# Modulation by per-column sums on VectorE, and unread matmuls on TensorE in three places of a two-model transformer kernel

## The chip, the cores and the metric

The kernel runs on one core of a Trainium2 chip. The metric is the device time of one execution in microseconds; for repeated executions the median is given. Before the change it is 2462.95 us, the median of three runs between 2461.41 and 2464.72 us.

## The reference, cut to what matters

The input is one sequence of 512 positions with 1024 features. It goes through a first model of two layers (banded attention, a gated short convolution, a SwiGLU feed-forward of width 2816) and then through one layer of a second model, here called the second block. That layer is modulated by a vector `c`:

```
c_act = jax.nn.silu(c)                              # c: 1 x 1024
mod = c_act @ ada_w[l] + ada_b[l]                   # ada_w: 1024 x 6144
sh_a, sc_a, gt_a, sh_m, sc_m, gt_m = split(mod, 6)
h = rmsnorm(x, norm_mix_g[l]) * (1.0 + sc_a) + sh_a
proj = h @ w_in[l]
```

`mod` depends on `c` and `ada_w` alone, so it can be computed at any time before the second block. It is 48 columns of 128 values in the kernel's layout.

## The kernel before

**Tiling.** Activations stand features by positions: 128 features on the partitions, 512 positions in a row. Every weight matrix is cut into units of 128 x 1024 (512 KB), 382 in all. A unit is loaded as `raw` on the queue of SyncE (line 255), cast by ScalarE to its high half `wh` (line 267), and VectorE subtracts to get the low half `wl` (line 268). `mm_kb` multiplies in three matmuls: high x high, high x low, low x high (lines 523 to 525). A unit serves 24 matmuls of 512 columns. `Stream.next` splits two units ahead of use. All of these tiles come from one pool, `blkp`, of 39 buffers; PSUM has eight banks, handed out in a fixed cycle by `ps`.

**Order.** The program lists its steps; a scheduler orders each engine's instructions by program order and by simulated times, and each engine then executes its list in order, waiting where data is missing. `order` (line 374 uses it for table loads) adds a dependency without a semaphore.

**Modulation.** `ada_start` computes silu(c) at the start from small VectorE instructions and one Exp. `ada_step` is called twice in each of the iterations 2 to 13 of the first model's feed-forward loop, in both layers, 48 times in all. Each step loads the next block of `ada_w` (128 rows of one sixth, 512 KB, `adaraw`, line 934) and multiplies the present one by a scalar per partition, adding into `adaacc` (lines 918 and 920). After every eighth step, eight matmuls with the tile of ones as moving operand sum `adaacc` over the partitions (line 927; each is executed as two passes, one column each), and VectorE adds the bias into `mod` (line 930).

**The crossing.** Between two stages that need a norm over all features, `cross` works in two halves of 256 positions: `tail(0)`, `chain(0)`, `tail(1)`, then the first half's normalised input, `chain(1)`, and `Head`, the first matmuls of the next stage, half by half. For the second block the chain is `chain2`: `rstd` sums squares over the partitions with one-column matmuls (tile `pc`, line 416), GpSimd takes the power -0.5, `bcast` spreads the result with one matmul against a diagonal (tiles `dg`, `pb`, lines 427 and 431), the residual is added and squared, and `rstd` and `bcast` run a second time for the pre-norm. PE has little else to do while a half's chain runs. `b2_masks` loads constants (line 968) and casts them on VectorE (line 971, tile `pastr`) right after the crossing in program order.

**The start.** `setup` issues the first loads and sets a 128 x 128 tile of ones (line 357). PE's first instruction comes when the first weight unit and input block are loaded and split.

Of the kernel before, what the change touches and what calls it, by code (L numbers as in the profile page):

```python
# [14 lines left out]
P = 128  # L15
T = 512
D = 1024
NB = 8
# [14 lines left out]
def col_layout():  # L33
    off, lay = 0, {}

    def add(name, n):
        nonlocal off
        lay[name] = (off, n)
        off += n

    for l in range(DEPTH):
        for n in ("g_pre_mix", "g_post_mix", "g_pre_ffn", "g_post_ffn"):
            add(f"{n}{l}", NB)
        add(f"conv_w{l}", 3 * NB)
        add(f"sink{l}", NH)
    for n, c in (("c", NB), ("ada_b", 48), ("nmg", NB), ("nfg", NB), ("fcw", 3 * NF), ("fcb", NF), ("dgq", 1),
                 ("dgk", 1), ("lam", P), ("subg", 1), ("fgq", 1), ("fgk", 1), ("fbf", 4), ("ngq", 1), ("ngk", 3),
                 ("pe", 32)):
        add(n, c)
    return lay, off  # L50
# [32 lines left out]
def pack(inp):  # L83
# [47 lines left out]
    for l in range(DEPTH):  # L131
# [4 lines left out]
    setc("c", fm_cols(inp["c_2"][0]))  # L136
# [39 lines left out]
    for i in range(2):  # L176
# [20 lines left out]
        "ada": np.asarray(inp["ada_w_2"])[0].reshape(NB, P, 6, U).transpose(2, 0, 1, 3).reshape(48, P, U),  # L197
# [82 lines left out]
class Kern:  # L280
# [31 lines left out]
    def small(self, name, shape, dt=F32, bufs=3):  # L312
        return self.smp.tile(shape, dt, name=self.n(name), tag=name, bufs=bufs)

    TAIL = 4
    NHF = 4
    NH3 = 4
# [20 lines left out]
    def setup(self):  # L338
        nc = self.nc
        self.cols = self.cpool.tile([P, self.ncol], F32, name="cols")  # L340
        nc.sync.dma_start(self.cols[:, :NB], self.a["cols"][:, :NB])
        xin = self.a["x"].rearrange("p (j a t) -> p j a t", j=4, a=2)
        self.xsrc = [[xin[:, j, :, t0:t1] for j in range(4)] for t0, t1 in HV]
        self.xpre = {}
        self.st.load_to(1)
        for j in range(4):
            self.xpre[0, j] = self.xload(0, j)
        self.st.load_to(3)
        self.cst = self.cpool.tile([P, 520], F32, name="cst")
        nc.sync.dma_start(self.cst, self.a["consts"])  # L350
        nc.sync.dma_start(self.cols[:, NB:], self.a["cols"][:, NB:])
        self.ident = self.cst[:, 0:P]
        self.band = self.cst[:, P:512]
        self.caus = self.cst[:, 384:512]
        self.valid = self.cst[:, 512:520]
        self.ones = self.cpool.tile([P, P], F32, name="ones")
        nc.vector.memset(self.ones, 1.0)
        self.mhalf = self.cpool.tile([P, 4], F32, name="mhalf")
        nc.vector.memset(self.mhalf, -0.5)
        self.R = self.cpool.tile([P, T], F32, name="R")  # L360
# [47 lines left out]
    def rstd(self, acc, hv, acc_tail=None):  # L408
        nc = self.nc
        n = (hv[1] - hv[0]) // P  # L410
        pc = self.ps("pc")
        parts = [acc[:, a, hv[0]:hv[1]] for a in range(2)] if len(acc.shape) == 3 else [acc[:, hv[0]:hv[1]]]
        parts += acc_tail if acc_tail else []
        for j, a in enumerate(parts):
            for i in range(n):
                nc.tensor.matmul(pc[:, i:i + 1], a[:, i * P:(i + 1) * P], self.ones[:, 0:1],
                                 start=j == 0 and i == 0, stop=j == len(parts) - 1 and i == n - 1)
        v = self.small("rs_v", [P, 4])[:, :n]
        r = self.small("rs_r", [P, 4])[:, :n]
        nc.vector.tensor_scalar(v, pc[:, :n], 1.0 / D, EPS, op0=OP.mult, op1=OP.add)  # L420
        self.rstd_small(v, r, n)
        return r

    def bcast(self, r, n=4):
# [6 lines left out]
        nc.tensor.matmul(pb[:, :n * P], self.ones, dg[:, :n * P], start=True, stop=True)  # L431
        return pb

    def add_sq(self, acc, src, first, eng):
# [24 lines left out]
        self.nc.sync.dma_start(d, t)  # L459
        self.xdst[hi][j] = d  # L460

    def cross(self, tail, chain, head, fin, early=0):
        self.xdst = [[None] * 4 for _ in range(2)]
        if tail:
            tail(0)
# [1 line left out]
        post0 = chain(0)  # L467
        if tail:
            tail(1)
        post0()  # L470
        post1 = chain(1)
        head.run(0)
# [45 lines left out]
    def mm_kb(self, ps, w, h, kb, first, last, wk=None, hv=(0, T)):  # L518
# [6 lines left out]
        nc.tensor.matmul(ps[:, t], w[1][:, sl], h.hi[kb][:, t], start=False, stop=last)  # L525

    def mblock(self, h):
        w = self.st.next()
# [364 lines left out]
        return F  # L893

    def ada_start(self):
        nc = self.nc
        self.ca = self.cpool.tile([P, NB], F32, name="ca")
        o, _ = self.lay["c"]
        c = self.cols[:, o:o + NB]
        self.sigmoid_small(self.ca, c, [P, NB])  # L900
        nc.vector.tensor_mul(self.ca, self.ca, c)
        self.mod = self.cpool.tile([P, 48], F32, name="mod")
        self.ada_i = 0
        self.ada_raw = None

    def ada_step(self):
        nc = self.nc
        i = self.ada_i
        if i >= 48:
            return  # L910
        self.ada_i += 1
        if i == 0:
            self.ada_load(0)
        t = self.ada_raw
        g, kb = divmod(i, NB)
        if kb == 0:
            self.ada_acc = self.blk("adaacc", [P, U], F32)
            nc.vector.tensor_scalar(self.ada_acc, t, self.ca[:, 0:1], None, op0=OP.mult)
        else:
            nc.vector.scalar_tensor_tensor(self.ada_acc, t, self.ca[:, kb:kb + 1], self.ada_acc, op0=OP.mult,  # L920
                                           op1=OP.add)
        if i + 1 < 48:
            self.ada_load(i + 1)
        if kb == NB - 1:
            ps = self.ps("ada")
            for m in range(NB):
                nc.tensor.matmul(ps[:, m:m + 1], self.ada_acc[:, m * P:(m + 1) * P], self.ones[:, 0:1], start=True,
                                 stop=True)
            o = self.lay["ada_b"][0] + g * NB
            nc.vector.tensor_add(self.mod[:, g * NB:(g + 1) * NB], ps[:, :NB], self.cols[:, o:o + NB])  # L930

    def ada_load(self, i):
        self.ada_raw = self.blk("adaraw", [P, U], F32)
# [45 lines left out]
    def chain2(self, i, pend, h, G, sh, xs=None, acc2=None, sq2=None):  # L979
# [3 lines left out]
        if pend:  # L983
# [10 lines left out]
        pb = self.bcast(self.rstd(acc2, HV[i], sq2), 2)  # L994
        R = self.half("Rp")
        nc.scalar.copy(R, pb[:, :256])

# [194 lines left out]
    def block2(self, tail, pend):  # L1192
# [5 lines left out]
        self.cross(tail, lambda i: self.chain2(i, pend, h, self.G1, 0, acc2=acc2), head, lambda i: None)  # L1198
        self.b2_masks()
        o = FM(self, "o2", NB, F32)  # L1200
        lo_h, hi_h = slice(0, 64), slice(64, 128)
# [580 lines left out]
```

## Time and profile before

| | us |
|---|---|
| median of three runs | 2462.95 |
| lowest, highest | 2461.41, 2464.72 |
| the profiled execution | 2465.88 |
| its span, first to last instruction | 2464.2 |
| PE busy in it | 2407.3 |
| DVE busy in it | 1324.1 |
| ACT busy in it | 996.1 |
| POOL busy in it | 399.2 |

PE is TensorE's matmuls, PEld its weight loads, DVE VectorE, ACT ScalarE, POOL GpSimd, SP SyncE, on whose queue all loads stand. A busy time is the union of an engine's instructions. A matmul's duration is that of one instruction from issue to its end; since matmuls overlap in the array, the distance between two starts is the time that one takes from the stream. A clock of 1.00 is the granted TensorE clock of 2.4 GHz, 0.50 that of 1.2 GHz. Times in the traces count from the span's start.

### The profile page before, as it was taken

The numbers are of one execution on the slowest core, as the hardware profiler recorded it, in microseconds if no ns is written. First come the engines' busy times: TensorE is split into PE (matmuls) and PEld (weight loads), VectorE is DVE, ScalarE is ACT, GpSimd is POOL, SyncE is SP. The second block draws the span as 40 slices with busy tenths as digits, with TensorE's granted clock in tenths as the row PEclk, the third lists the DMA queues.
The fourth block names the chain that finished last, engine by engine and source line by source line (L and its number), as shares of the span: only waits on it lengthen the run. The fifth ranks groups of instructions, "written<-read, shape, count | busy, mean of one in ns | idle before, by whom it ended". The sixth has DMA issues, their size and how long they took to land.

```text
span 2464.2 us, 32671 instructions
## 1 busy us (share of the span) xinstructions
PE 2407.3 (98%) x12680; PEld 2073.7 (84%) x12680; DVE 1324.1 (54%) x2324; ACT 996.1 (40%) x1808; POOL 399.2 (16%) x437
## 2 busy tenths in 40 slices
PE   8999999999999999999999999999898899999999
PEld 8888888888888898888888888888788878888888
DVE  6777544366533177775434655422667586644531
ACT  4555423442223245554224322322375575333420
POOL 3433001211110034230012111100021232000000
PEclk9999999999999999999999999999799999999999
DMA  4511523355423244223233553332221204233350
GB/s 159 149 61 64 165 94 103 103 196 200 149 85 121 80 144 126 69 83 99 94 98 129 181 195 137 99 107 74 91 88 53 83 22 146 78 103 103 105 171 24
DMA packets 90115, 272.77 MB, mean 111 GB/s; under 512 B 10175, under 2 KB 19007, under 8 KB 89960
## 3 DMA queue, kind: packets, MB, share of 16 engines
q1 hardware_dynamic: 89960, 270.68, 33.1%
q8 instruction: 100, 1.64, 0.3%
q14 instruction: 55, 0.45, 0.1%
HBM read 249.65 MB, written 15.22 MB: 107 GB/s over the span
## 4 chain that ended last, share of the span: by engine, by line
PE 90%; DVE 3%; ACT 3%; POOL 2%; issue 2%; DMA 0%; SPq 0%; POOLq 0%; ACTq 0%; DVEq 0%
PE ps L523 24%; PE ps L525 24%; PE ps L524 24%; PE hd L524 2%; PE hd L525 2%; PE hd L523 2%; PE o L840 2%; PE pt L815 1%; PE tm L1025 1%; PE tm L1026 1%; PE tm L1027 1%; POOL t L576 1%; POOL t L575 1%; ACT pp L378 1%; PE s L791 1%
## 5 line engine op out<-in xcount | busy, mean ns | idle before, releaser
L268 DVE TENSOR_TENSOR wl<-raw,wh 128x1024 fp32r<-128x1024 f32 x382 | 477.5, 1267 | 346.6 <-ACT wh L267 283.2
L267 ACT CAST wh<-raw 128x1024 fp32r<-128x1024 f32 x382 | 390.0, 1050 | 188.6 <-DMA raw<-in_w_dram 99.0
L525 PE MATMUL ps<-hh,wl 128*128 128x512 f32 x752 | 295.3, 393 | 0.9 <-DVE wl L268 0.8
L524 PE MATMUL ps<-hl,wh 128*128 128x512 f32 x752 | 294.9, 392 | 0.0
L523 PE MATMUL ps<-hh,wh 128*128 128x512 f32 x752 | 294.4, 392 | 0.0
L524 PE MATMUL ps<-hfl,wh 128*128 128x512 f32 x640 | 249.3, 390 | 0.0
L523 PE MATMUL ps<-hfh,wh 128*128 128x512 f32 x640 | 249.1, 390 | 0.0
L525 PE MATMUL ps<-hfh,wl 128*128 128x512 f32 x640 | 248.9, 389 | 0.0
L525 PEld LDWEIGHTS ps<-hh,wl 128*128 128x128 f32 x752 | 141.3, 188 | 29.1 <-DVE wl L268 2.1
L524 PEld LDWEIGHTS ps<-hl,wh 128*128 128x128 f32 x752 | 141.2, 188 | 27.2
L523 PEld LDWEIGHTS ps<-hh,wh 128*128 128x128 f32 x752 | 141.2, 188 | 27.1 <-ACT ot L844 0.2
L525 PE MATMUL ps<-hidh,wl 128*128 128x512 f32 (+1 forms) x396 | 145.1, 366 | 0.0
L523 PE MATMUL ps<-hidh,wh 128*128 128x512 f32 (+1 forms) x396 | 144.9, 366 | 0.0
L524 PE MATMUL ps<-hidl,wh 128*128 128x512 f32 (+1 forms) x396 | 144.7, 365 | 0.0
L378 ACT ACTIVATE pp<-pp,at_nm 128x256 f32<-128x256 f32 (+1 forms) x208 | 114.4, 553 | 68.2 <-DVE at_nm L797 60.0
L525 PEld LDWEIGHTS ps<-hfh,wl 128*128 128x128 f32 x640 | 120.1, 188 | 24.9
L524 PEld LDWEIGHTS ps<-hfl,wh 128*128 128x128 f32 x640 | 120.2, 188 | 24.7
L523 PEld LDWEIGHTS ps<-hfh,wh 128*128 128x128 f32 x640 | 120.0, 188 | 24.8
L720 POOL TENSOR_TENSOR gs<-gs,R 128x512 f32<-128x512 f32 x44 | 71.4, 1623 | 377.6 <-ACT gs L378 366.6
L524 PE MATMUL ps<-h3l,wh 128*128 128x512 f32 x320 | 124.5, 389 | 0.0
L525 PE MATMUL ps<-h3h,wl 128*128 128x512 f32 x320 | 124.5, 389 | 0.0
L523 PE MATMUL ps<-h3h,wh 128*128 128x512 f32 x320 | 124.3, 389 | 0.0
(461 smaller groups left out, 5200.3 us busy)
## 6 DMA issues: line engine op xcount, KB each, us to landing
raw<-in_w_dram SPq DMA_DIRECT2D x382, 512.0 KB, 3.7
adaraw<-in_ada_dram SPq DMA_DIRECT2D x48, 512.0 KB, 5.6
xd<-xh SPq DMA_DIRECT2D x24, 256.0 KB, 2.1
xh<-xd SPq DMA_DIRECT2D x24, 256.0 KB, 3.1
xh<-in_x_dram SPq DMA_DIRECT2D x16, 256.0 KB, 5.0
Q<-ql SPq DMA_DIRECT2D x32, 128.0 KB, 3.4
bias_d<-row_d SPq DMA_DIRECT2D x8, 320.0 KB, 7.5
KH<-kst SPq DMA_DIRECT2D x16, 128.0 KB, 3.9
```

The lines of the kernel that those rows point to most:

```text
L267: nc.scalar.copy(hi, raw)
L268: nc.vector.tensor_sub(lo, raw, hi.bitcast(F32))
L378: i = nc.scalar.activation(out, in_, func, **kw)
L523: nc.tensor.matmul(ps[:, t], w[0][:, sl], h.hi[kb][:, t], start=first, stop=False)
L524: nc.tensor.matmul(ps[:, t], w[0][:, sl], h.lo[kb][:, t], start=False, stop=False)
L525: nc.tensor.matmul(ps[:, t], w[1][:, sl], h.hi[kb][:, t], start=False, stop=last)
L575: nc.gpsimd.tensor_mul(t2, t2, S)
L576: nc.gpsimd.tensor_add(t1, t1, t2)
L720: nc.gpsimd.tensor_mul(g, g, self.R)
L791: nc.tensor.matmul(ps[:, :n], q, KL[g][:, LO[i]:HI[i]], start=False, stop=True)
L815: nc.tensor.transpose(bank[:, c0:c0 + P], pslice(h, i)[:, c:c + P], self.ident)
L840: nc.tensor.matmul(ps[:, c0:c1], V[j][:, g * P:(g + 1) * P], t[b][:, a, c0:c1], start=(a == 0 and j == 0), stop=(a == 1 and j == 2))
```

## The change

The modulation is computed the other way round. `ada_w` is stored transposed, one block per column of `mod`: 128 outputs on the partitions, the 1024 inputs in a row. The row of c is loaded with a copy on every partition (`crow`), passed through Silu on ScalarE, and each step is one VectorE instruction that multiplies a block by it, sums along the row and adds the bias. The matmuls over `adaacc` and the small instructions for silu(c) go. The row is loaded and passed through Silu at step 0 and again at step 24, in the second layer, where the first block of the 24 is loaded afresh too.

Besides, matmuls whose results nothing reads are put on PE: eleven of 128 columns in `setup`, after the tile of ones; six of 256 columns behind `tail(1)` of the crossing into the second block; five of 256 columns behind the second broadcast of that crossing's second half. Each place takes a PSUM bank `pw`.

```diff
+        "ada": np.ascontiguousarray(np.asarray(inp["ada_w_2"])[0].T.reshape(48, P, U)),
+        "crow": np.ascontiguousarray(np.asarray(inp["c_2"])[0].reshape(1, U)),
...
+    WARM = 11
...
         nc.vector.memset(self.ones, 1.0)
+        ps = self.ps("pw")
+        for i in range(self.WARM):
+            nc.tensor.matmul(ps[:, :P], self.ones, self.ones, start=True, stop=True)
...
         if tail:
             tail(1)
+        if fill:
+            self.fill(self.pw, fill)
         post0()
...
+    def fill(self, ps, n):
+        prev = self.pe
+        for _ in range(n):
+            i = self.nc.tensor.matmul(ps[:, 0:256], self.ones, self.cst[:, 0:256], start=True, stop=True)
+            self.order(i, prev)
+            prev = i
...
-        if i == 0:
-            self.ada_load(0)
+        if i % 24 == 0:
+            self.ca = self.blk("ca", [P, U], F32)
+            self.nc.sync.dma_start(self.ca, self.a["crow"].to_broadcast([P, U]))
+            self.act(self.ca, self.ca, AF.Silu)
+            self.ada_load(i)
         t = self.ada_raw
-        g, kb = divmod(i, NB)
-        if kb == 0:
-            self.ada_acc = self.blk("adaacc", [P, U], F32)
-            nc.vector.tensor_scalar(self.ada_acc, t, self.ca[:, 0:1], None, op0=OP.mult)
-        else:
-            nc.vector.scalar_tensor_tensor(self.ada_acc, t, self.ca[:, kb:kb + 1], self.ada_acc, op0=OP.mult,
-                                           op1=OP.add)
-        if i + 1 < 48:
+        if i % 24 < 23:
             self.ada_load(i + 1)
-        if kb == NB - 1:
-            ps = self.ps("ada")
-            for m in range(NB):
-                nc.tensor.matmul(ps[:, m:m + 1], self.ada_acc[:, m * P:(m + 1) * P], self.ones[:, 0:1], start=True,
-                                 stop=True)
-            o = self.lay["ada_b"][0] + g * NB
-            nc.vector.tensor_add(self.mod[:, g * NB:(g + 1) * NB], ps[:, :NB], self.cols[:, o:o + NB])
+        o = self.lay["ada_b"][0] + i
+        self.nc.vector.tensor_tensor_reduce(out=t, in0=t, in1=self.ca, scale=1.0, scalar=self.cols[:, o:o + 1],
+                                            op0=OP.mult, op1=OP.add, accum_out=self.mod[:, i:i + 1])
...
+        k = int(pend is not None)
+        pb = self.bcast(self.rstd(acc2, HV[i], sq2, (0, 0)[i] * k), 2, (0, 5)[i] * k)
...
+        self.pw = self.ps("pw")
+        self.cross(tail, lambda i: self.chain2(i, pend, h, self.G1, 0, acc2=acc2), head, lambda i: None, fill=6)
```

## Rows read from the trace of the kernel before

**Rows 1.** The page: busy time of each engine, share of the span, instructions.
```profile
PE 2407.3 (98%) x12680; PEld 2073.7 (84%) x12680; DVE 1324.1 (54%) x2324; ACT 996.1 (40%) x1808; POOL 399.2 (16%) x437
```

**Rows 2.** The page: the chain that ended last, shares of the span by engine.
```profile
PE 90%; DVE 3%; ACT 3%; POOL 2%; issue 2%; DMA 0%; SPq 0%; POOLq 0%; ACTq 0%; DVEq 0%
```

**Rows 3.** Busy us of PE, PEld, DVE, ACT, POOL, then clock, DMA share, GB/s: first FFN.
```profile
490.00:620.00 130.00, 128.35 (x692) 111.21 (x691) 86.69 (x114) 44.66 (x70) 18.89 (x15) 1.00 0.54 196
```

**Rows 4.** Timeline of PE around one modulation group: start us, us, instruction.
```profile
569.48 0.39 PE L523 MATMUL ps<-hfh,wh 128*128 128x512 f32 x1
569.71 1.84 PE L927 MATMUL ada<-ones,adaacc 128*128 128x1 f32 x16
571.41 0.49 PE L524 MATMUL ps<-hfl,wh 128*128 128x512 f32 x1
571.74 0.40 PE L525 MATMUL ps<-hfh,wl 128*128 128x512 f32 x1
```

**Rows 5.** Tile ada: durations in ns min/median/max, first and last start.
```profile
L927 PE MATMUL ada<-ones,adaacc x96: 164/250/250, 569.7 to 1519.6; 128*128 128x1 f32 x96
L930 DVE TENSOR_TENSOR mod<-ada,cols x6: 165/166/167, 571.6 to 1519.9; 128x8 f32<-128x8 f32 x6
```

**Rows 6.** DVE by line and shape: count, busy us, mean ns, idle before.
```profile
L920 DVE SCALAR_TENSOR_TENSOR adaacc<-adaraw,ca,adaacc 128x1024 f32<-128x1024 f32 x42 | 61.9, 1474 | 0.0
L918 DVE TENSOR_SCALAR adaacc<-adaraw,ca 128x1024 f32<-128x1024 f32 x6 | 4.5, 748 | 0.0
L1145 DVE CUSTOM_DVE_ANT_0 pp<-s,F 128x512 f32<-128x512 f32 x16 | 10.8, 677 | 0.0
L1145 DVE CUSTOM_DVE_ANT_0 pp<-s,F 128x256 f32<-128x256 f32 x16 | 6.6, 415 | 0.0
```

**Rows 7.** Stretches of the start, columns as in rows 3.
```profile
6.86:18.85 11.99, 11.42 (x49) 10.69 (x49) 11.87 (x35) 11.99 (x26) 1.63 (x1) 1.00 0.99 352
18.85:30.00 11.15, 11.15 (x93) 11.10 (x93) 8.04 (x16) 5.42 (x8) 0.48 (x1) 1.00 0.73 251
```

**Rows 8.** Timeline of the start: the tile that the early matmuls read.
```profile
0.90 0.17 DVE L357 MEMSET ones<- 128x128 f32 x1 [0.90 <-PEq L1773]
```

**Rows 9.** Stretches of the crossing into the second block, columns as in rows 3.
```profile
1722.90:1726.80 3.90, 0.22 (x3) 0.03 (x1) 3.56 (x6) 2.54 (x6) 0.00 (x0) 0.84 0.71 236
1735.80:1742.60 6.80, 6.33 (x28) 6.04 (x29) 6.39 (x21) 3.71 (x9) 0.80 (x1) 0.50 0.01 2
1763.80:1770.00 6.20, 6.20 (x29) 6.20 (x30) 5.72 (x18) 2.27 (x7) 0.00 (x0) 0.50 0.09 24
```

**Rows 10.** Timeline of PE in the same crossing.
```profile
1726.78 1.87 PE L416 MATMUL pc<-ones,acc 128*128 128x1 f32 x8 [3.68 <-DVE acc L443]
1731.88 1.19 PE L431 MATMUL pb<-dg,ones 128*128 128x256 f32 x2 [3.23 <-DVE dg L427]
1759.63 1.12 PE L431 MATMUL pb<-dg,ones 128*128 128x256 f32 x2 [1.64 <-DVE dg L427]
1763.78 1.22 PE L523 MATMUL hd<-h2h,wh 128*128 128x256 f32 x4 [3.02 <-ACT h2h L515]
```

**Rows 11.** Tile pb: durations in ns min/median/max of its matmul passes.
```profile
L431 PE MATMUL pb<-dg,ones x40: 378/379/765, 22.8 to 2106.1; 128*128 128x256 f32 x40
```

**Rows 12.** Timeline of DVE in the first wait of the crossing.
```profile
1731.10 0.29 DVE L971 CAST pastr<-consts 128x256 fp32r<-128x256 f32 x1 [2.26 <-DMA consts<-in_consts_dram]
```

**Rows 13.** The page: a DMA queue, a DMA issue (KB, landing us); tile adaraw: issues.
```profile
q1 hardware_dynamic: 89960, 270.68, 33.1%
bias_d<-row_d SPq DMA_DIRECT2D x8, 320.0 KB, 7.5
L934 SPq DMA_DIRECT2D adaraw<-in_ada_dram x48: 328/385/1257, 530.8 to 1493.4; - x48
```

**Rows 14.** Timeline: one weight split on DVE and its first use on PE.
```profile
540.12 1.49 DVE L268 TENSOR_TENSOR wl<-raw,wh 128x1024 fp32r<-128x1024 f32 x1 [1.04 <-ACT wh L267]
543.87 0.39 PE L525 MATMUL ps<-hfh,wl 128*128 128x512 f32 x1
```

More of the change, by code (lines that the diff above doesn't have):

```diff
@@ L45, in col_layout @@
         add(f"sink{l}", NH)
-    for n, c in (("c", NB), ("ada_b", 48), ("nmg", NB), ("nfg", NB), ("fcw", 3 * NF), ("fcb", NF), ("dgq", 1),
+    for n, c in (("ada_b", 48), ("nmg", NB), ("nfg", NB), ("fcw", 3 * NF), ("fcb", NF), ("dgq", 1),
                  ("dgk", 1), ("lam", P), ("subg", 1), ("fgq", 1), ("fgk", 1), ("fbf", 4), ("ngq", 1), ("ngk", 3),
@@ L135, in pack @@
         setc(f"sink{l}", np.tile(inp["attn_sink"][l][None, :], (P, 1)))
-    setc("c", fm_cols(inp["c_2"][0]))
     setc("ada_b", fm_cols(inp["ada_b_2"][0]))
@@ L196, in pack @@
         "phi": phib.reshape(P, 32 * P),
-        "ada": np.asarray(inp["ada_w_2"])[0].reshape(NB, P, 6, U).transpose(2, 0, 1, 3).reshape(48, P, U),
+        "ada": np.ascontiguousarray(np.asarray(inp["ada_w_2"])[0].T.reshape(48, P, U)),
+        "crow": np.ascontiguousarray(np.asarray(inp["c_2"])[0].reshape(1, U)),
         "x": np.ascontiguousarray(np.asarray(inp["x"])[0].T.reshape(NB, P, T).transpose(1, 0, 2).reshape(P, NB * T)),
@@ L406, in rstd_small, with rstd @@
         nc.vector.tensor_mul(r, r, s)
-    def rstd(self, acc, hv, acc_tail=None):
+    def rstd(self, acc, hv, acc_tail=None, fill=0):
         nc = self.nc
@@ L415, in rstd @@
             for i in range(n):
-                nc.tensor.matmul(pc[:, i:i + 1], a[:, i * P:(i + 1) * P], self.ones[:, 0:1],
+                self.pe = nc.tensor.matmul(pc[:, i:i + 1], a[:, i * P:(i + 1) * P], self.ones[:, 0:1],
                                  start=j == 0 and i == 0, stop=j == len(parts) - 1 and i == n - 1)
+        if fill:
+            self.fill(self.pw, fill)
         v = self.small("rs_v", [P, 4])[:, :n]
@@ L422, in rstd, with bcast @@
         return r
-    def bcast(self, r, n=4):
+    def bcast(self, r, n=4, fill=0):
         nc = self.nc
@@ L430, in bcast @@
         pb = self.ps("pb")
-        nc.tensor.matmul(pb[:, :n * P], self.ones, dg[:, :n * P], start=True, stop=True)
+        self.pe = nc.tensor.matmul(pb[:, :n * P], self.ones, dg[:, :n * P], start=True, stop=True)
+        if fill:
+            self.fill(self.pw, fill)
         return pb
@@ L460, in xstore, with cross @@
         self.xdst[hi][j] = d
-    def cross(self, tail, chain, head, fin, early=0):
+    def cross(self, tail, chain, head, fin, early=0, fill=0):
         self.xdst = [[None] * 4 for _ in range(2)]
@@ L469, in cross @@
             tail(1)
+        if fill:
+            self.fill(self.pw, fill)
         post0()
@@ L524, in mm_kb @@
         nc.tensor.matmul(ps[:, t], w[0][:, sl], h.lo[kb][:, t], start=False, stop=False)
-        nc.tensor.matmul(ps[:, t], w[1][:, sl], h.hi[kb][:, t], start=False, stop=last)
+        self.pe = nc.tensor.matmul(ps[:, t], w[1][:, sl], h.hi[kb][:, t], start=False, stop=last)
+    def fill(self, ps, n):
[4 more added lines that the diff above has]
+            prev = i
     def mblock(self, h):
@@ L895, in ada_start @@
     def ada_start(self):
[L896 to L901, printed above, removed]
         self.mod = self.cpool.tile([P, 48], F32, name="mod")
         self.ada_i = 0
-        self.ada_raw = None
     def ada_step(self):
-        nc = self.nc
         i = self.ada_i
@@ L1197, in block2 @@
         acc2 = self.blk("acc2", [P, 2, T], F32)
-        self.cross(tail, lambda i: self.chain2(i, pend, h, self.G1, 0, acc2=acc2), head, lambda i: None)
+        self.pw = self.ps("pw")
+        self.cross(tail, lambda i: self.chain2(i, pend, h, self.G1, 0, acc2=acc2), head, lambda i: None, fill=6)
         self.b2_masks()
```

1 line of the change is left out of this document (removed).

## The prediction

> **What bounds the kernel now.** Read the page's busy times first: TensorE (PE) is busy 98% of the span, VectorE (DVE) 54% [rows 1]. Then the chain that ended last: 90% of it is PE work [rows 2]. So time is taken out by removing PE work or by making it faster, stage by stage. In the first feed-forward stretch (490 to 620 us), where half of the modulation is computed, PE is busy 128.35 of 130 us at clock 1.00, with DVE at 86.69 and ScalarE (ACT) at 44.66: PE sets the pace, the others have slack [rows 3]. At the start DVE is as full as PE, 11.87 against 11.42 of 11.99 us [rows 7]. In the crossing into the second block PE waits for others, 3.68, 3.23, 1.64 and 3.02 us [rows 10], and then runs two stretches of 6.80 and 6.20 us at granted clock 0.50, the 1.2 GHz level [rows 9].
>
> **Part 1, modulation by VectorE sums.** Removed from PE: six groups of 16 passes with one column each, 96 in all [rows 5]. Price of one group: the 512-column matmul before starts at 569.48 and the group's first pass at 569.71, so a matmul takes 0.23 us there; the next matmul starts at 571.41 instead of 569.71, 1.70 us late, and its successor at 571.74, 0.33 later instead of 0.23, so 1.80 us in all [rows 4]. PE waits for nothing in that stretch [rows 3], so the whole price is on the path: 6 x 1.80 = **10.8 us**. DVE loses 42 multiply-adds (61.9 us), 6 multiplies (4.5 us) and 6 small adds (6 x 0.166 = 1.0 us): 67.4 us [rows 5, 6]. It gains 48 multiply-and-sum instructions of 1024 columns. The trace has that form at 256 and 512 columns, 415 and 677 ns; each 256 columns cost 262 ns, so 1024 take about 677 + 2 x 262 = 1201 ns, together 57.6 us, plus a short read of each sum [rows 6]. DVE does not get heavier, and it was not the limit; I count nothing.
>
> Added are two loads that spread the row of c over 128 partitions (512 KB, SyncE's queue ahead of the first modulation load) and two Silu on ACT that wait for them; ada block 24 is no longer loaded ahead. Behind the Silu on ACT stand the casts of the next weights, behind the first sum on DVE their low halves, and PE waits for those. Silu over 1024 columns costs ACT about as much as a weight cast, which has slack. The only repeated-row transfers in the trace take 7.5 us for 320 KB [rows 13]. The cover at its tightest: a weight split ends at 540.12 + 1.49 = 541.61 and is first used at 543.87, 2.3 us later [rows 14]. The split waited 1.04 us for its cast on ACT, so the cast ran from about 539.1 [rows 14]. The new load can start where the first modulation load did, 530.8 [rows 13]. At 7.5 us it lands at 538.3, a Silu as long as that cast ends about 539.3, and the cast is 0.2 us late, covered by 2.3. If landing grows with size, 7.5 x 512/320 = 12 us, the loss is 12 - 7.5 + 0.2 - 2.3 = 2.4 us. Range 0 to 2.4 per place; I take 0.3 in all.
>
> **Part 2, eleven matmuls at the start.** They read only the tile of ones, ready at 0.90 + 0.17 us [rows 8]. Eight one-column passes of the same tile at clock 0.50 take 1.87 us, 0.234 each [rows 10]; with two passes per matmul the 22 passes take about 5.1 us, until 6.2, before the first useful matmul at 6.86 (where the first stretch of rows 7 begins). They delay nothing. What they may bring: from 6.86 to 18.85 PE executes 49 instructions in 11.42 us, from 18.85 on 93 in 11.15 [rows 7]. The clock column shows 1.00 in both. By the column the early matmuls are worth 0; by the pace the first stretch ran at half speed, and at the later pace (0.12 us) its 49 take 5.9 us, 5.5 less. The Trainium skill ("TensorE: Matmul & The Clock Gate", What's actually happening) says that the array's clock starts throttled and that activity releases it. This agrees with the instruction counts, and not with the column; by the column alone the sum would be 1.2 us smaller. The 5.5 are not all to be had: DVE, which makes the low halves, is full there [rows 7]. Nor is it sure that the burst suffices: in the crossing the clock rose only after 6.80 and 6.20 us of near-continuous work [rows 9], longer than 5.1 us, and after the burst come useful matmuls with gaps. Bounds 0 and 5.5; I take **1.2**, nearer the bottom, where those two rises point. Seven short DVE instructions of the old sigmoid also go, about 7 x 0.166 = 1.2 us [rows 5], on a full engine; inside the bounds.
>
> **Part 3, six matmuls in the first wait.** One pass of 256 columns of this kind lasts 379 ns at full clock and 765 at half [rows 11]; two in a row take 1.19 us at half, so the second starts 0.42 after the first, and 0.21 at full [rows 10]. A matmul is two passes: 0.43 or 0.85. Six are 2.6 us at full clock, from about 1722.9 to 1725.5, inside the wait that ends at 1726.78. The eight sums there then run at full clock, about 0.9 instead of 1.87 us. But the broadcast after them (1731.88) is not set by them: DVE sits 2.26 us on a cast that waits for a load of constants until 1731.10, with the operand of the broadcast queued behind it [rows 12]. And 4 us of idleness again precede 1731.88. I count **0.2**, bounds 0 and 1.5 (the sums' 0.9 and a faster broadcast's 0.6).
>
> **Part 4, five matmuls in the second wait.** They follow the broadcast at 1759.63; the half-array after it starts at 1763.78 [rows 10]. At half clock the broadcast takes 0.85 and the five 5 x 0.85 = 4.25 us: end at 1764.7, **0.95 late**. For that PE is busy from 1759.63 instead of 1763.78. With rises 6.20 to 6.80 us after work sets in [rows 9] the clock is full at 1765.8 to 1766.4 rather than 1770.0. Before, 6.2 us at half do 3.1 us of full-clock work; now 1.1 to 1.7 us at half do 0.55 to 0.85, and the other 2.25 to 2.55 follow at full: caught up at 1768.4 to 1768.7, 1.3 to 1.6 us ahead. If the clock holds through the wait, the five end by 1762.2, before 1763.78, and 3.1 are won. If the clock ignores them, 0.95 is lost. PE has work without a gap there [rows 9], so what it wins is kept. I take **2.0**.
>
> **Sum.** 10.8 + 1.2 + 0.2 + 2.0 - 0.3 = 13.9 us. Against the profiled execution (2465.88 us, span 2464.2 and 1.7 around it) that is 2452.0; this execution is 2.9 above the median of the runs, 2462.95, so the median comes to **2449 us**, 0.56% less. What ends last then is PE again.
>
> **Rivals.** (a) *The clock doesn't follow:* parts 2 to 4 give between -0.95 and +0.5; 9.5 to 11.0 us remain, 2452 to 2453.5. For it: the burst is shorter than both rises [rows 9]. Against: in part 4 the work before the rise gets longer whatever rule the clock follows. (b) *The freed time becomes waits on weights:* the 2.3 us of cover [rows 14] is used up at both places where c is loaded and part of the 10.8 comes back as waits of PE, 3 to 6 us: 2452 to 2455, and with (a) up to 2459. (c) *Everything pays:* 10.8 + 5.5 + 1.5 + 3.1, less DVE's limit at the start of some 2 to 3: about 2444. (d) *Slower:* the Silu holds ACT, and so the weight casts, until the row of c has landed. With landing time L the loss per place is about L - 9.5 us (12 gave about 2.5), so both places eat the 13.9 us from L = 16.5 on. If the load ran on one DMA engine: the queue moved 270.68 MB in 33.1% of 16 engines' span, 20.7 GB/s per engine [rows 13], and 512 KB take 25 us: 2 x 15.5 = 31 us lost, about 2480. The Trainium skill ("DMA: Bandwidth & Descriptors", Rules for kernel authors) warns that a small or repeating outermost dimension confines a load to that few engines; here the outermost dimension written is the 128 partitions, so its own condition isn't met. (e) *The change doesn't do what it says:* were the 96 passes free where they stand, part 1 would be 0 and 2460 would follow; rows 4 show the delay, so I give it almost nothing.
>
> **How the numbers follow.** Forecast (2445.5 to 2452) 0.66; (a) 0.17; (b) 0.08; (c) 0.05; (d) 0.03; (e) 0.01. The range from 2444 to 2456 takes in (a), most of (b) and half of (c), and 1.6 us of spread between the runs; some 0.15 stays outside. 0.2% (4.9 us) is about what a measurement of this kernel can tell from no change. Faster by more (under 2458): forecast, (a), (c) and most of (b), 0.92. Within: the rest of (b) and (e), 0.04. Slower: (d) and what I don't see, 0.04.
>
> **What would show it.** No PE pass on a tile ada, and the 512-column matmuls at 0.23 us throughout 490 to 620 us (part 1); PE waits on wl or wh there mean (b) or (d). Matmuls of 256 columns 0.12 us apart before 18.85 (part 2). The broadcast still at about 9 us after the last tail matmul, behind the constants' load (part 3). After the second broadcast, the half-array's matmuls at 0.12 us apart some 2 to 4 us sooner than 6.2 us after their start (part 4). The prediction is wrong if PE's waits in the two feed-forward stages grow by more than 3 us, or if the useful matmul after the five starts over 1 us later and stays at half clock as long as before.

## The result, and the profile after

The changed kernel takes 2448.23 us (median of four runs, 2444.53 to 2449.39); the kernel before, beside it, 2463.84 us (2461.41 to 2466.24). The ratio is 0.9934 with a 95% interval of 0.9917 to 0.9951: 15.6 us less, where 13.9 were forecast. The time lies in the predicted range and 0.8 us from the predicted value. That doesn't make every step right: two of the four parts were badly sized, in opposite directions. The profiled execution took 2449.39 us, span 2447.7.

The page of the kernel after, the busy times and the chain that ended last, which answer to [rows 1] and [rows 2]:

```profile
PE 2402.3 (98%) x12628; PEld 2068.1 (84%) x12628; DVE 1326.6 (54%) x2359; ACT 997.2 (41%) x1809; POOL 387.2 (16%) x437
PE 90%; DVE 3%; ACT 3%; POOL 2%; issue 2%; DMA 0%; SPq 0%; POOLq 0%; ACTq 0%; DVEq 0%
```

The chain has the same shares as before. PE's busy time falls by only 5.0 us, because the fills count as busy; where the time went can't be read from the sums of a page. It is read from the same marks in both traces. Each number below is the distance between the starts of two matmuls in the timeline of PE, the first one that from the start of the span to the start of a matmul:

| stretch, us | before | after |
|---|---|---|
| start of the span to the last matmul on `pv`, first layer | 44.5 | 43.6 |
| last `tp` to last `hfh` matmul (FFN), layer 0 | 252.3 | 248.2 |
| the same, layer 1 | 253.6 | 248.0 |
| first wait of the crossing: last tail matmul to first `hd` on `h2h` | 12.9 | 10.6 |
| first to last `hd` on `h2h` (holds the second wait) | 43.2 | 39.5 |
| last `z` to last `tm` | 144.1 | 145.9 |

The rows hold stretches at granted clock 0.50 that differ between executions of one kernel. Before, layer 1 has one of 3.4 us in its FFN and layer 0 none; after, both have one of 3.4 us. The last row is no loss by the change: a second profile of the changed kernel (e5_again, below) shows 142.7 there.

In the FFNs no matmul on a tile `ada` is left, and PE waits for no weight that it didn't wait for before. The new operations of the modulation, from the views of the tiles `adaraw` and `ca` (durations in ns min/median/max, first and last start), which answer to [rows 6]:

```profile
L930 DVE CUSTOM_DVE_ANT_0 adaraw<-adaraw,ca,cols x48: 1266/1274/2317, 542.2 to 1501.9; 128x1024 f32<-128x1024 f32 x48
L923 SPq DMA_DIRECT2D ca<-in_crow_dram x2: 432/432/433, 530.9 to 1381.8; - x2
L382 ACT ACTIVATE ca<-ca x2: 1054/1056/1058, 536.9 to 1387.8; 128x1024 f32<-128x1024 f32 x2
```

The load of the row of c is issued at 530.9 and Silu starts at 536.9, without a wait on ACT: the row has landed within 6.0 us. In rival (d) a loss needed more than 9.5. Nobody waits for the sums. Each new VectorE instruction is followed by a read of its sum, 78 ns in the median, so the 48 take about 65 us where the old ones took 67.4.

The first wait in the timeline of the kernel after (start us, us, engine, line, instruction), which answers to the first two lines of [rows 10] and to [rows 12]:

```profile
1711.95 2.75 PE L540 MATMUL pw<-cst,ones 128*128 128x256 f32 x12
1715.78 1.05 PE L420 MATMUL pc<-ones,acc 128*128 128x1 f32 x8 [1.08 <-DVE acc L451]
1717.83 0.43 DVE L433 TENSOR_TENSOR dg<-cst,rs_r 128x256 f32<-128x256 f32 x1 [0.80 <-POOL rs_r L402]
1718.41 1.19 PE L437 MATMUL pb<-dg,ones 128*128 128x256 f32 x2 [1.57 <-DVE dg L433]
1720.01 0.29 DVE L972 CAST pastr<-consts 128x256 fp32r<-128x256 f32 x1 [1.75 <-DMA consts<-in_consts_dram]
1722.46 0.79 PE L533 MATMUL hd<-h2h,wh 128*128 128x256 f32 x2 [0.53 <-ACT h2h L525]
```

The surprise stands in lines 3 and 5. Before, VectorE waited for the constants, made the cast [rows 12] and only then `dg`, in the trace of the kernel before:

```profile
1731.31 0.42 DVE L427 TENSOR_TENSOR dg<-cst,rs_r 128x256 f32<-128x256 f32 x1
```

Now `dg` comes first and the cast after it. The broadcast `pb` no longer waits for the constants: it comes 6.6 us after the last tail matmul, where the prediction had "about 9". And the clock falls all the same: `pb` takes 1.19 us, as long as before.

The second wait, which answers to the last two lines of [rows 10], and the 10.2 us after its `pc`, columns as in [rows 3]:

```profile
1742.72 0.95 PE L420 MATMUL pc<-ones,acc 128*128 128x1 f32 x8
1745.30 0.67 PE L437 MATMUL pb<-dg,ones 128*128 128x256 f32 x2 [1.63 <-DVE dg L433]
1745.81 2.32 PE L540 MATMUL pw<-cst,ones 128*128 128x256 f32 x10
1748.99 0.74 PE L533 MATMUL hd<-h2h,wh 128*128 128x256 f32 x4 [0.86 <-ACT h2h L525]
1742.70:1752.90 10.20, 7.49 (x50) 6.57 (x49) 7.07 (x22) 2.14 (x7) 0.69 (x1) 1.00 0.18 67
```

Here the clock stays at 1.00 through the wait. The ten passes of the five fills end at 1748.1, before the half-array's matmuls at 1748.99.

### The profile page after: what moved, and what is told of

The parts are those of the page before. It is cut to its first block, busy times and chain, and to the rows that moved or that the text cites. A ratio compares the mean times of both kernels' runs of the same rounds, so it can differ in the third digit from the quotient of the medians.

```text
span 2447.7 us, 32535 instructions
## 1 busy us (share of the span) xinstructions
PE 2402.3 (98%) x12628; PEld 2068.1 (84%) x12628; DVE 1326.6 (54%) x2359; ACT 997.2 (41%) x1809; POOL 387.2 (16%) x437
## 4 chain that ended last, share of the span: by engine, by line
PE 90%; DVE 3%; ACT 3%; POOL 2%; issue 2%; DMA 0%; SPq 0%; POOLq 0%; ACTq 0%; DVEq 0%
PE ps L535 24%; PE ps L533 24%; PE ps L534 24%; PE hd L534 2%; PE hd L535 2%; PE hd L533 2%; PE o L857 2%; PE tm L1027 1%; PE pt L832 1%; PE tm L1029 1%; PE tm L1028 1%; POOL t L593 1%; POOL t L592 1%; ACT pp L382 1%; PE s L808 1%
## 5 line engine op out<-in xcount | busy, mean ns | idle before, releaser
L268 DVE TENSOR_TENSOR wl<-raw,wh 128x1024 fp32r<-128x1024 f32 x382 | 484.4, 1285 | 349.4 <-ACT wh L267 278.8
L737 POOL TENSOR_TENSOR gs<-gs,R 128x512 f32<-128x512 f32 x44 | 63.5, 1442 | 375.7 <-ACT gs L382 364.8
```

The costliest lines, as they stand in the source:

```text
L268: nc.vector.tensor_sub(lo, raw, hi.bitcast(F32))
L737: nc.gpsimd.tensor_mul(g, g, self.R)
```

## The experiments

The ratios stand against the kernel before, run beside each set: its median was 2464.88 us for e1 to e4, 2464.82 for e5 to e8 and 2463.62 for e9 to e11. The last three columns are marks of the profiled execution, as in the table above; where the text says that `pv` ends, it gives the start of its last matmul.

| kernel | median us (lowest to highest) | ratio, 95% interval | last `pv` | first wait | `hd` on `h2h` |
|---|---|---|---|---|---|
| e1_ada_only | 2453.11 (2449.98 to 2455.24) | 0.9948, 0.9934 to 0.9962 | 43.1 | 12.9 | 41.8 |
| e2_warm_only | 2453.54 (2452.95 to 2454.78) | 0.9956, 0.9943 to 0.9968 | 43.8 | 12.9 | 41.0 |
| e3_one_fill | 2451.89 (2447.46 to 2452.19) | 0.9942, 0.9929 to 0.9954 | 44.3 | 10.7 | 41.2 |
| e4_no_five | 2451.47 (2450.73 to 2451.88) | 0.9946, 0.9934 to 0.9959 | 43.1 | 10.3 | 43.1 |
| e5_again | 2447.03 (2444.41 to 2450.38) | 0.9932, 0.9919 to 0.9944 | 44.7 | 10.6 | 39.7 |
| e6_passes_back | 2459.77 (2457.48 to 2462.23) | 0.9982, 0.9974 to 0.9991 | 45.0 | 10.4 | 40.8 |
| e7_more | 2450.64 (2447.50 to 2451.97) | 0.9943, 0.9931 to 0.9956 | 44.3 | 13.0 | 39.6 |
| e8_more_ffn | 2461.44 (2457.57 to 2463.61) | 0.9985, 0.9976 to 0.9994 | 44.8 | 11.3 | 42.0 |
| e9_no_start | 2448.07 (2445.27 to 2449.37) | 0.9931, 0.9916 to 0.9945 | 44.7 | 10.5 | 39.9 |
| e10_ffn_fills | 2447.46 (2446.37 to 2450.65) | 0.9931, 0.9918 to 0.9944 | 44.0 | 10.7 | 40.9 |
| e11_both_waits | 2449.99 (2445.96 to 2451.32) | 0.9938, 0.9923 to 0.9952 | 43.0 | 11.5 | 40.0 |

One kernel's executions differ by up to 5 us, so a whole time separates two neighbours of a ladder badly; the marks within a stage do it to some tenths.

**The modulation alone.**

```diff
-    WARM = 11
+    WARM = 0
...
-        pb = self.bcast(self.rstd(acc2, HV[i], sq2, (0, 0)[i] * k), 2, (0, 5)[i] * k)
+        pb = self.bcast(self.rstd(acc2, HV[i], sq2, (0, 0)[i] * k), 2, (0, 0)[i] * k)
...
-        self.cross(tail, lambda i: self.chain2(i, pend, h, self.G1, 0, acc2=acc2), head, lambda i: None, fill=6)
+        self.cross(tail, lambda i: self.chain2(i, pend, h, self.G1, 0, acc2=acc2), head, lambda i: None, fill=0)
```

> The modulation by VectorE sums alone: no unread matmuls at the start, none in the crossing. Theory A (the 96 one-column passes lay on the path and nothing takes their place): 10.8 us faster than the kernel before less 0.3, about 2453; each FFN of the first block (from the end of its tp matmuls to the last matmul on hfh, 252.3 and 253.6 us before) is shorter by 5.4; the first wait of the crossing (last tail matmul to first hd matmul) stays at 12.8 us and the second keeps its time. Rival B (the freed TensorE time makes weight loads or DVE late, and half of it is given back): 5 us or less, about 2458, with new waits of PE on wh or wl in the FFNs. Rival C (part of the changed kernel's gain in the crossing comes from the new modulation, not from the fills): the first wait is shorter than 12.8 by over 0.5 here too.

Measured 2453.11 us, as theory A says; the first wait is 12.9, so rival C falls. The FFNs take 248.3 and 247.0 us.

**Plus the eleven matmuls at the start** (`WARM = 11` again).

> As the kernel with the modulation alone, plus the 11 unread matmuls at the start. Theory A: the start is DVE's, the clock rises earlier but falls back to half from about 10 to 17 us, so the last pv matmul of the first layer ends at 43.6 instead of 44.5 us: 0.9 us, about 2452. Rival D (the 0.9 is no effect of these matmuls but the difference of two executions): pv ends within 0.3 us of 44.5. Rival E (all of the half-speed time of the start is won): 4 to 5 us, about 2448.

`pv` ends at 43.8 us. That is nearest to theory A, but the kernel without these matmuls ended it at 43.1, and the time is 0.4 us longer, not 0.9 shorter. E falls; between A and D two profiles don't decide, so the start was undone by itself (e9_no_start, below).

**Plus one of the six fills** (`fill=1`).

> As the kernel with modulation and start matmuls, plus a single fill of the six in the first wait and none of the five. With one fill the order of VectorE already has the diagonal dg ahead of the cast of the mask constants, as in the changed kernel, while TensorE is hardly busier in the wait. Theory F (most of what the first wait gained is this order): last tail matmul to first hd matmul 11.1 us (12.8 less 1.7), the 8 one-column passes pc still at about 1.9 us, about 2450. Rival G (the gain is the clock's: the fills keep it at full speed): 12.6 or more, with one fill as without, about 2452.

The first wait in both kernels, first e2_warm_only, then e3_one_fill:

```profile
1717.44 1.87 PE L420 MATMUL pc<-ones,acc 128*128 128x1 f32 x8 [3.67 <-DVE acc L451]
1719.35 0.16 DVE L426 TENSOR_SCALAR rs_v<-pc 128x2 f32<-128x2 f32 x1 [1.96 <-PE pc L420]
1721.71 0.29 DVE L972 CAST pastr<-consts 128x256 fp32r<-128x256 f32 x1 [2.20 <-DMA consts<-in_consts_dram]
1721.92 0.42 DVE L433 TENSOR_TENSOR dg<-cst,rs_r 128x256 f32<-128x256 f32 x1
1722.48 1.19 PE L437 MATMUL pb<-dg,ones 128*128 128x256 f32 x2 [3.17 <-DVE dg L433]
1726.37 0.79 PE L533 MATMUL hd<-h2h,wh 128*128 128x256 f32 x2 [0.36 <-ACT h2h L525]
```

```profile
1713.88 1.05 PE L420 MATMUL pc<-ones,acc 128*128 128x1 f32 x8 [3.24 <-DVE acc L451]
1714.97 0.16 DVE L426 TENSOR_SCALAR rs_v<-pc 128x2 f32<-128x2 f32 x1 [1.14 <-PE pc L420]
1715.93 0.42 DVE L433 TENSOR_TENSOR dg<-cst,rs_r 128x256 f32<-128x256 f32 x1 [0.80 <-POOL rs_r L402]
1716.50 1.19 PE L437 MATMUL pb<-dg,ones 128*128 128x256 f32 x2 [1.57 <-DVE dg L433]
1718.22 0.29 DVE L972 CAST pastr<-consts 128x256 fp32r<-128x256 f32 x1 [1.86 <-DMA consts<-in_consts_dram]
1720.67 0.79 PE L533 MATMUL hd<-h2h,wh 128*128 128x256 f32 x2 [0.64 <-ACT h2h L525]
```

One fill, 0.5 us of work for PE, turns the scheduler's list for VectorE around, and with it the wait falls from 12.9 to 10.7. From `rs_v` to `pb` there are 1.53 us instead of 3.13: 1.6. The sums `pc` run at full speed here, 0.8 us. In return the cast now stands just ahead of `hn`: from `Rp` at 1717.73 to `hn` at 1718.43, 0.70 instead of 0.41, so 0.3 is given back. Together 2.1. Theory F holds, but its bound on `pc` was wrong: the sums had full speed with a single fill, since the clock fell only at 1714.9, a microsecond after they began. Whether the one fill or chance put the fall there, one profile doesn't show. In the kernel with the modulation alone it fell in the middle of them (they took 1.41 us) and the wait was 12.9 all the same: while the cast is ahead of `dg`, faster sums gain nothing, as the prediction said. The Trainium skill ("DVE: scalar operands, raw-bit mode, write accounting and state across instructions", Flops that outlive an instruction) calls VectorE's queue one in-order queue; the trace agrees, since `rs_r`, the last input of `dg`, was done on GpSimd at 1720.28 and `dg` stood behind the cast until 1721.92.

**All six, but none of the five** (`fill=6`, the second tuple `(0, 0)`). The instruction lists of this kernel, of the one before and of the changed kernel are the same but for the fills and one swapped pair on VectorE and one on ScalarE, so this is the cleanest step of the ladder.

> The changed kernel without the five fills of the second wait. Theory H (the five fills keep the clock at full speed behind them): the clock falls in the second wait, the last hd matmul on h2h comes 39.4 plus 2 to 3.7 us after the first (39.4 in the changed kernel), about 2451 against 2448. Rival I (the second half gained because the first is now earlier and at full speed, not by the five fills): 39.4 within 0.5 us, and the time of the changed kernel. Against the kernel with one fill, the first wait shows the other five of the six fills alone: theory F expects 10.5 here, about 0.8 less than with one fill, from the 8 passes pc at full speed (1.05 us instead of 1.87).

First the second wait here, then its 10.2 us from the broadcast on, columns as in [rows 3]:

```profile
1746.92 1.19 PE L437 MATMUL pb<-dg,ones 128*128 128x256 f32 x2 [1.63 <-DVE dg L433]
1751.14 1.22 PE L533 MATMUL hd<-h2h,wh 128*128 128x256 f32 x4 [3.02 <-ACT h2h L525]
1746.90:1757.10 10.20, 7.15 (x30) 6.46 (x31) 8.24 (x25) 3.12 (x9) 0.00 (x0) 0.50 0.04 13
```

The clock is at 0.50 for all of the 10.2 us, PE executes 30 instructions in them, and `hd` takes 43.1 us against 39.5: theory H, 3.6 us in this pair. Of these, 2.7 lie behind the second `pb` (from it to the last `hd` 19.3 us here, 16.6 in the changed kernel); the rest lies ahead of it, where both kernels have the same fills and the half-speed stretch begins 6.8 us after the last tail matmul here, 4.9 there. The other five of the six fills bring 0.4 us in the first wait (10.7 to 10.3); over the six profiles with six fills and nothing else in that wait the mean is 10.5.

**The changed kernel again.**

> The changed kernel once more, for a second profile of it. Theory H (the five fills hold the clock): no half-speed stretch between the first hd matmul on h2h plus 10 us and the last, first to last 39.5 us as in its first profile; in the four profiles without the five fills, the kernel before included, the clock fell there each time. Rival J (its absence was an accident of one execution): a stretch at half speed near 23 to 35 us after the first hd matmul, 41 to 43 us. For the start: if the 11 unread matmuls gain nothing, the last pv matmul ends anywhere from 43.1 to 44.5.

39.7 us, no half-speed stretch in the second wait, 2447.03 us; rival J falls for this pair. With the later runs it gets a limit: of the seven profiles with the five fills (e8 is left out, since the order around them is another one there; it has 6.8 us at half speed from ahead of the fills on) two, e6 and e10, show a stretch of 3.4 us there, the others show none; all five without them show 6.8 to 10.2 us. Mean from first to last `hd`: 40.1 with (39.5, 39.7, 40.8, 39.6, 39.9, 40.9, 40.0), 42.1 without (43.2, 41.8, 41.0, 41.2, 43.1). The fills are worth 2.0 us. Counted from the second `pb` alone to the last `hd` it is 16.7 against 18.8, 2.1 us.

**The passes put back, unread.**

```diff
+        if i % 8 == 7:
+            ps = self.ps("ada")
+            for m in range(8):
+                self.nc.tensor.matmul(ps[:, m:m + 1], t[:, m * P:(m + 1) * P], self.ones[:, 0:1], start=True, stop=True)
         o = self.lay["ada_b"][0] + i
```

> The changed kernel with the 96 one-column passes put back: after every eighth step of the modulation, eight matmuls of one column on its tile, whose sums nothing reads. Theory A (their 10.8 us were on the path): 10.8 us slower than the changed kernel, about 2459, 5.4 in each FFN of the first block. Rival K (most of the gain came from the lighter VectorE and ScalarE work or from other transfers): under 4 us slower, about 2452.

12.7 us slower than the changed kernel beside it; rival K falls. One group in the timeline of this kernel, then the two FFN stages (columns as in [rows 3]) of this kernel, of the changed kernel and of e3_one_fill:

```profile
565.85 1.84 PE L932 MATMUL ada<-ones,adaraw 128*128 128x1 f32 x16
567.55 0.49 PE L533 MATMUL ps<-hfh,wh 128*128 128x512 f32 x1
567.87 0.40 PE L534 MATMUL ps<-hfl,wh 128*128 128x512 f32 x1
492.30:744.60 252.30, 250.64 (x1232) 212.40 (x1232) 148.88 (x199) 84.15 (x119) 34.18 (x25) 1.00 0.46 159
1348.30:1600.50 252.20, 250.53 (x1231) 212.33 (x1231) 148.86 (x199) 84.06 (x119) 34.19 (x25) 1.00 0.45 159
```

```profile
490.90:739.10 248.20, 246.54 (x1184) 208.57 (x1183) 148.79 (x199) 84.19 (x119) 34.16 (x25) 0.99 0.46 161
1341.60:1589.60 248.00, 246.34 (x1184) 208.37 (x1184) 148.90 (x199) 84.39 (x119) 34.17 (x25) 0.99 0.47 162
```

```profile
491.70:738.30 246.60, 244.94 (x1183) 206.91 (x1182) 148.68 (x198) 84.09 (x119) 34.15 (x25) 1.00 0.47 163
1340.90:1587.70 246.80, 245.14 (x1184) 207.01 (x1184) 148.72 (x199) 84.32 (x119) 34.15 (x25) 1.00 0.46 162
```

The x in the PE column falls by 48, three groups of 16. At clock 1.00 in both, 252.25 against 246.7: 5.55 us per layer, 11.1 in all, 1.85 per group. From the last `tp` to the last `hfh` matmul this kernel takes 252.3 us in both layers, as the kernel before does in layer 0 at the same clock, so the new VectorE work and the new loads add nothing there. The changed kernel shows 0.99 and 1.4 us more, a half-speed stretch of 3.4 us near 495 and 1345 that comes in most executions and not in all. The group costs the same as in [rows 4] with other data on its tile, and most of it is the passes' own pace: in both kernels the sixteen start within 1.59 us.

**Twelve more fills in the first wait.**

```diff
+            self.pe = pci
+            self.fill(self.pw, 5)
+            self.pe = pbi
+            self.fill(self.pw, 2)
...
-            pb = self.bcast(self.rstd(acc, HV[i], sqs[i]), 2)
+            pb = self.bcast(self.rstd(acc, HV[i], sqs[i], (0, 5)[i]), 2)
```

> The changed kernel with twelve more fills in the first wait: five after the passes pc of the first half, two after pb, five after the passes pc of the second half. Theory L (in the first wait the six fills end too early, the clock falls 4 us behind them and stays at half for the first 4.5 us of hd): the clock holds at full speed through the wait, pb takes 0.6 instead of 1.2 us, and hd runs at 0.12 us a pass from the start: the last hd matmul on h2h comes 2 us earlier after the last tail matmul than in the changed kernel (48.0 instead of 50.1), about 2446. Rival M (this stretch is VectorE's and ScalarE's, which make h2h and h2l): the clock holds, but the last hd matmul comes within 0.5 us of where it did. Rival N (the fills hold up pb or the next passes): first wait longer than 10.6.

```profile
1717.65 4.04 PE L545 MATMUL pw<-cst,ones 128*128 128x256 f32 x10
1718.79 0.42 DVE L433 TENSOR_TENSOR dg<-cst,rs_r 128x256 f32<-128x256 f32 x1 [0.80 <-POOL rs_r L402]
1721.48 0.69 PE L437 MATMUL pb<-dg,ones 128*128 128x256 f32 x2
```

Rival N, 13.0 us: the clock fell at 1718.3 in spite of the fills, ten passes took 4.04 us, and `pb`, whose operand was ready at 1719.2, started at 1721.48 behind them. Against the changed kernel 3.6 us are lost by the medians, 2.3 from the last tail matmul to the last `hd` (52.6 against 50.3). Not all of it is the clock: PE also waits 1.0 us on `wl` in `hd`, which the changed kernel doesn't, because the fills also move two weight casts on ScalarE and their low halves on VectorE back in the lists. An unread matmul in front of a useful one costs most just when the clock falls.

**The same, and three fills in each FFN crossing** (a bank `self.pw = self.ps("pw")` and `fill=3` in `ffn1`).

> As the kernel with twelve more fills, and three fills in each of the two FFN crossings of the first block, behind the last tp matmul, where a half-speed stretch of 3.4 to 6.8 us follows in most profiles. Theory O (these fills keep the clock up there): no stretch at half speed near 494 and 1345; each FFN stage (last tp to last hfh matmul) takes 246.7 us, which is what the profiles without the stretch show, instead of 248.1 to 249.5: 1.4 to 2.7 us each, about 2442. Rival P (the clock falls over the later gap of 1 us ahead of hfl, which these fills don't touch): 248 to 249.5 and about 0.3 us more each for the fills, about 2447.

The FFN stages take 247.1 us each and show no half-speed stretch: theory O for them. The first wait answers e7_more: with the same twelve fills the clock stayed at 1.00 through it, and the ten passes took 2.40 us instead of 4.04:

```profile
1716.74 2.40 PE L546 MATMUL pw<-cst,ones 128*128 128x256 f32 x10
```

So the clock's fall in e7_more is one of two outcomes. But even here the first wait is 11.3 us, longer than the changed kernel's 10.5 in the mean.

Yet the kernel takes 2461.44 us. The added bank shifts the turn in which `ps` hands out all later banks, and with it the order in block 2. PE's waits between 1723 and 1830 us (us in total, times, longest), which the changed kernel doesn't have:

```profile
PE pc L420 <- DVE acc L451: 3.3, 1, 3.3
PE z L1459 <- DVE rz L1472: 2.7, 1, 2.7
PE hd L541 <- DVE wl L268: 1.9, 1, 1.9
```

The first two are missing in e7_more, which has the twelve fills, and in e10 and e11, which have the FFN fills without the shift: that leaves the shift of banks, alone or together with the fills. The third comes also in e7 and e11, 1.0 us each, so it belongs to the fills of the first wait.

**The start undone** (`WARM = 0`, all else as changed).

> The changed kernel without its 11 unread matmuls at the start. Theory Q (they gain nothing; the start is set by the loads and by DVE, and its end varies by execution): the last pv matmul of the first layer ends between 43.1 and 45.0 us, as in the eight profiles with these matmuls (mean 44.2), and the time is that of the changed kernel, 2447 to 2448. Rival R (they gain the 1.2 us of the prediction): pv ends past 45.2 us, time 2449.

2448.07 us, `pv` ends at 44.7: theory Q. Without the matmuls the scheduler also swaps some early instructions on PE, VectorE and ScalarE, so this compares two whole starts, not eleven matmuls by themselves. The stretches of the start, columns as in [rows 3], first in the changed kernel, then in this one:

```profile
6.20:10.16 3.96, 2.21 (x12) 1.69 (x12) 3.88 (x7) 3.96 (x10) 0.00 (x0) 0.99 0.99 372
10.16:16.94 6.78, 6.47 (x29) 6.08 (x29) 6.53 (x21) 6.78 (x14) 0.69 (x1) 0.50 1.01 355
16.94:30.00 13.06, 13.06 (x110) 13.01 (x110) 9.70 (x17) 7.26 (x12) 0.69 (x1) 1.00 0.75 258
```

```profile
6.70:10.16 3.46, 2.94 (x8) 2.06 (x9) 2.72 (x7) 3.01 (x7) 0.00 (x0) 1.00 1.04 405
10.16:16.94 6.78, 6.68 (x31) 6.38 (x31) 6.68 (x21) 6.78 (x14) 1.61 (x1) 1.00 1.02 360
16.94:30.00 13.06, 13.06 (x102) 13.01 (x102) 10.23 (x17) 7.59 (x13) 0.83 (x1) 1.00 0.80 256
```

From 10.16 to 16.94 us PE executes 29 instructions with the early matmuls and 31 without them: half speed in both, whatever the column says (the trace of the second has no record of the clock before 19.0 us). Ahead of that the early matmuls do raise the clock: PE executes 12 instructions up to 10.16 us in 2.21 us of work instead of 8 in 2.94, but waits for VectorE between them.

**FFN fills without the shift of banks** (the bank in `ffn1` taken from the tag `mm` without a step of the cycle; `fill=3`).

> The changed kernel with three fills behind the last tp matmul in each FFN crossing of the first block, in a PSUM bank that doesn't shift the turns of the other tiles. Theory O (they keep the clock up in the FFNs): no half-speed stretch near 495 and 1346, last tp to last hfh matmul 247.0 us in both layers instead of 248.2, block 2 as in the changed kernel (first wait 10.6, hd on h2h 39.6, z after 4.9): 2.4 us faster, about 2445. Rival P (the FFNs gain, and block 2 gives it back, through other stretches at half speed): the FFN stages at 247.0, but the time within 1 us of 2447.5.

Both FFN stages take 246.8 us at clock 1.00, 1.2 to 1.4 each less than in the two profiles of the changed kernel (theory O). Over all kernels, none of the six FFNs with fills has a half-speed stretch, and twelve of the sixteen with the new modulation and without fills or passes have one. But the median is 2447.46: rival P. In its profile block 2 is slower than in e5_again: 40.9 against 39.7 in `hd`, 46.0 against 44.6 from first to last `z`, 145.2 against 142.7 from there to the last `tm`, each with a further stretch at half clock. The last of these is no sign of the fills, since the changed kernel's first profile has 145.9 there, and the profiled execution was the slowest of the five, 2450.65 us. Whether the earlier arrival brings these stretches or chance does, one profile can't tell; that stays open.

**Both.** (Three fills behind `pc`, one behind `pb`, two behind the second half's `pc`.)

> As the kernel with FFN fills, and in the first wait of the crossing three fills behind the passes pc of the first half, one behind pb, two behind the passes pc of the second half: half of what the kernel with twelve more had, cut to the gaps there by the 0.46 us that a fill took at full speed. Theory L: no fill holds up pb or hd, the first wait stays at 10.6 or becomes 0.6 shorter (pb at full speed), hd runs at full speed from its start, last tail to last hd matmul 48.2 instead of 50.1: about 2443. Rival M (VectorE and ScalarE set that stretch): 50.1 within 0.5, about 2445. Rival S (the clock falls at a point of its own, fills or not, as it did in the kernel with twelve more, where ten passes of fills took 4.04 us): a half-speed stretch within 10 us of the last tail matmul, 50.1 or more.

Rival S: the clock fell 6 us after the last tail matmul, the last two fills (four passes in 2.05 us) held `hd` up, first wait 11.5 us, 2449.99 us. PE waits 1.0 us on `wl` in `hd` here too. No version here beats the changed kernel by more than its runs differ.

## Why the prediction came true, step by step

**Part 1 (forecast 10.8 less 0.3; measured 11.1).** Right, and shown three ways: the modulation alone brings 11.8 us by the medians, the passes put back cost 12.7, and the stage shows 5.55 per layer at equal clock. The price of a group read from four lines, 1.80, measured 1.85. The 0.3 for the load and Silu was not needed: 6.0 us to land, no wait on ACT. The new VectorE form takes 1274 ns, not the 1201 extrapolated from its shorter shapes; with slack beside it that cost nothing.

**Part 2 (forecast 1.2; measured 0).** Wrong, though the profile after seems to confirm it: `pv` ended 0.9 us earlier. In ten profiles with the early matmuls it ends between 43.0 and 45.0 us, mean 44.1; in three without them between 43.1 and 44.7, mean 44.1. By the spread of the ten, the standard error of such a difference of means is about 0.45 us. The step that failed is the choice of a value inside the bounds 0 and 5.5, and its reason, a burst perhaps too short, is not what happened. The burst of 5.1 us did raise the clock, to 1.00 for 3.4 us in all ten profiles, but it fell again at 8.2 to 10.2 us, behind the gaps of the first useful matmuls, of which the step had warned too. It then rose for good at 16.0 to 19.3 us. Without the burst it did so at 16.1, 18.9 and 19.0, no later, and the end of `pv` goes with that rise: 43.0 to 43.8 where it came by 17.1 us, 44.0 to 45.0 where it came after 18. The Trainium skill ("TensorE: Matmul & The Clock Gate", What's actually happening) says that the number of slow matmuls at a start varies from run to run of one kernel; the two profiles of the changed kernel agree, with that rise at 16.9 and 18.7 us and `pv` ending at 43.6 and 44.7.

**Part 3 (forecast 0.2, bounds 0 and 1.5; measured 2.3).** The step that failed is "the operand of the broadcast queued behind it": it took VectorE's order in the wait as given. The fills are also input to the scheduler, and one of them is enough to put `dg` ahead of the cast. That is 1.6 of the 2.3, with 0.8 from the sums, which count only in the new order, and 0.3 given back at `hn`. What the fills do by the clock alone, over one fill, is 0.2 (10.7 to the mean of 10.5). The second half of the reasoning held: in all six of these profiles the clock fell 0.2 to 2.7 us after the last of the sums had started, and in four of them `pb` ran at half speed throughout (1.17 to 1.19 us), as before.

**Part 4 (forecast 2.0; measured 2.0 in the mean).** Right, and both of its cases occur. In five of seven profiles the clock doesn't fall at all, the case put at 3.1; it brought 2.7 against e4_no_five, the kernel that differs by the five fills alone, and less against kernels whose stretch was shorter. In two it falls and rises sooner, after 3.4 us instead of 6.8 to 10.2, the case put at 1.3 to 1.6; from `pb` to the last `hd` they take 17.1 and 17.0 us, 1.7 to 1.8 less than the 18.8 without the fills. The loss of 0.95 shows in none: in e6 and e10, where the fills ran in part at half speed, `hd` started 4.22 and 4.16 us after `pb`, against 4.15 in [rows 10].

**The sum.** 11.1 + 0 + 2.3 + 2.0 = 15.4 us, against 15.6 and 17.8 by the medians of the two sets of runs. The forecast, rather than one of the rivals, is what happened; rival (a) is refuted by part 4, (b), (d) and (e) by part 1, and (c) by part 2, which gave nothing of its 5.5. That 2449 lay so close to 2448.23 is in part luck: it owes something to two errors of opposite sign.

## What to carry to other kernels

Read the price of an operation on a full engine from the distance between its neighbours' starts; it held here to 3%. Where a scheduler orders the engines' lists, an edit on one engine can reorder another: compare the order of the instructions on every engine around the edit before costing it at "nothing". Work that only keeps the clock up pays where it ends before the next useful matmul is ready, and is judged over several profiles, since one execution's half-speed stretches move by more than the effect.

## What the runs showed of the hardware that was not expected

- At clock 1.00 the passes of a fill (128x256, f32) start 0.22 us apart (twelve within 2.75 us in all), the matmuls of 256 columns on `fp32r` operands 0.12. A fill of two passes costs almost as much as four of the kernel's own matmuls.
- Half-speed stretches come with work on PE close by: in e7_more the clock fell at 1718.3 us, 0.65 after fills had begun and after PE had been busy 3.7 of the 4.8 us before them; in e8_more_ffn it stayed at 1.00 with the same fills. Near 495 and 1345 us one and the same kernel has 3.4 us of it or, in others with the same FFN, none or 6.8, each 3.4 worth 1.2 to 1.5 us.
- At the start the granted-clock column shows 1.00 while PE executes at half pace (31 instructions in 6.78 us), and shows 0.50 for the same pace in another execution; there the pace is the better witness. Without the early matmuls the traces hold no record of the clock before it first rises (16.1 to 19.0 us).
